# Two-layer Fourier and attention block on one core: a norm's chain, column operations, the special columns' product and a fourth weight buffer

## The chip, the core and the metric

The kernel runs on one core of a Trainium2 chip. The core has five engines, each with an instruction queue of its own: TensorE (PE, matrix products; its weight loads are shown as PEld), VectorE (DVE), ScalarE (ACT), GpSimd (POOL) and SyncE (SP, which here only issues DMAs). On-chip memory is SBUF, and products are accumulated in eight banks of PSUM. The metric is the device time of one execution in microseconds.

## The reference, cut to what matters

Two layers work on 256 tokens `x` and 256 context tokens `ctx`, each of 2048 features. Layer 0 is a Fourier mixer on both, layer 1 is windowed attention. All is float32.

```python
shift, scale, gate = split(silu(c) @ ada_w[i] + ada_b[i], 3)
h = rmsnorm(x, norm_g[i]) * (1 + scale) + shift            # the same for ctx with c_ctx
# layer 0:
u, z = split(h @ w_in, 2)                                   # 4096 features each
ug = u.reshape(b, n, 16, 256)                               # 16 groups of 256 features
f = fft2(ug, axes=(tokens, group features), norm='ortho').real
f = einsum('bngc,gcd->bngd', f, w_mix).reshape(b, n, 4096)
y = f * silu(z)
x = x + gate * (y @ w_out[0])
# layer 1: the same with attention in place of the Fourier branch, then a final rmsnorm
```

The change lies in layer 0, in the first 200 us of the time.

## The kernel before, in words

**Numbers in halves.** Each float32 operand is split into two parts of a shorter float type: `split` (lines 60 to 62) copies the high part on ACT (L61) and subtracts it on DVE (L62). `mm3` (L73 to L76) makes three products, high by high (L74), high by low (L75), low by high (L76).

**The opening** (L331 to L379). Four blocks of 128 rows `xn` are loaded: two of `x` (s = 0), two of `ctx` (s = 1). `square` sums squares, one half of the features on ACT, the other on DVE. `xsplit(t, c)` splits 512 features of block t. `turn_x` transposes a block pair on PE into PSUM (L236), where the first call takes all eight banks, and `copy_x` copies the banks out, even ones on DVE (L244), odd ones on ACT (L242). `norm(s)` (L196 to L208) adds the sums (L200), takes the inverse root in `rsqrt` (L78 to L87: L82 on DVE, the power on POOL in L83, three small DVE steps), scales the table `dm` of the token transform into the splits `dh` (ACT, L205) and `dl` (DVE, L206), and copies the root to `rr` (L207). `dft(s, c)` then makes the transform over tokens with `dh` and `dl` as the moving side (L74 to L76, `ps<-dh,xs`). `ada` (L249 to L254) makes pieces of the modulation from `awp`, 1 MB loads; `turn` (L261 to L273) turns them and writes the scale `gs0` (L271) and the shift `sh0` (L269).

**The z products** (L390 to L441), four steps of four feature tiles k. `z_x(k)` scales the turned tokens (L303), makes the split of the modulated tokens on ACT (L304) and DVE (L305, `zl_end`); `z_step(k)` multiplies them by the weights of the first six blocks of z. `hx_prep(k)` (L316 to L328) makes `hx`, the split of the token transform for the u products (L322 on ACT, L323 on DVE), and puts the value with the shift in it into column 0 (`f0` in L324, then L326 and L327). At the end the six sums go through Silu (L440) to memory as `zd`, on POOL's queue.

**The sixteen groups** (L483 to L553). `load_u(g)` loads the two 1 MB halves of group g's folded weights (`raw`, L47), forms differences and sums (`wm` in L123, L124) and splits them (`wml`, `wmh`, `wpl`, `wph`) into eight tiles of pool `wfp`. `load_m(g)` loads the group's mixing matrix `m` (group 0 on POOL's queue, others on ACT's), forms `mt` (L458, L459), and multiplies it by the feature transform tables `ch`, `cl`. `part` multiplies `hx` by the group's weights: part m (48 products of 256 columns), then part p (48 of 260). `mix` joins the results of the group before. In group 0 the special columns (features 0 and 128 of every group, `wsp`, 32 in all) are multiplied by `hx` once: 16 tiles, three products each, with 32 stationary columns (L514 to L518); their result goes into `asp` (L519 to L521), which `mix` reads. `load_m(0)` is written ahead of this loop (L479).

**Buffers.** Loads of weights go through `raw`, three buffers of 8 KB a partition (L35), in the opening also through two more (`raw_st`). Pools that are opened with `reuse_waits="tile"` lie where closed pools lay, and their tiles wait for the tiles that lay there before. `ext` (14 tiles of 2 KB) holds splits of the z products and the Silu results until they are stored.

**The order of the work.** The text is one stream. A planner with a time model of its own puts each engine's instructions in an order when the program is built: what the model finds ready first, earlier text before later. `tc.issue_after(ins)` adds that instructions of the same engine as `ins`, written in its block, stand behind `ins` in that engine's queue; instructions of other engines in the block are not bound. On the chip each queue runs strictly in that order.

Of the kernel before, what the change touches and what calls it, by code (L numbers as in the profile page):

```python
# [29 lines left out]
def tile_dit(ctx: ExitStack, tc: tile.TileContext, a: dict, out: bass.AP):  # L30
# [21 lines left out]
    def act(dt=F32):  # L52
        return actp.tile([P, 512], dt, tag="act", name="act")
# [24 lines left out]
    def rsqrt(pool, src, w, tag):  # L78
# [3 lines left out]
        V.tensor_scalar(v, src, 1.0 / D, EPS, op0=ALU.mult, op1=ALU.add)  # L82
# [52 lines left out]

    def load_u(g):
        return [split_uh(*f) for f in [load_uh(g, kh) for kh in range(2)]]
# [13 lines left out]
    with tc.tile_pool(name="st", reuse_waits="tile", bufs=1, side="right") as st, ExitStack() as sts:  # L151
# [44 lines left out]
        def norm(s):  # L196
# [4 lines left out]
            r = rsqrt(st, s2, 2, f"r{s}")  # L201
# [94 lines left out]
        zl_end = [None]  # L296

        def z_x(k):
            h, l = ext(F32R), ext(F32R)
            for s in range(2):  # L300
# [4 lines left out]
                zl_end[0] = V.scalar_tensor_tensor(l[:, q], t, sh0[:, k, s : s + 1], h[:, q].bitcast(F32), op0=ALU.add, op1=ALU.subtract).ins  # L305
# [10 lines left out]
        def hx_prep(k):  # L316
            i, kk = k // 2, k % 2
            h, l = act(F32R), act(F32R)
            for s in range(2):
# [4 lines left out]
                V.scalar_tensor_tensor(f0[:, k, s : s + 1], rw[:, 0:1], gs0[:, k, s : s + 1], sh16[:, k, s : s + 1], op0=ALU.mult, op1=ALU.add)  # L324
            h, l = (x.rearrange("p (s j) -> p s j", s=2) for x in (h, l))
            V.tensor_copy(h[:, :, 0], f0[:, k, :])  # L326
            V.tensor_tensor(l[:, :, 0], f0[:, k, :], h[:, :, 0].bitcast(F32), op=ALU.subtract)  # L327
# [8 lines left out]
        norm(0)  # L336
        xsplit(1, 0)
        for kp in range(4):
            copy_x(0, kp, ox[kp])
        xsplit(1, 1)  # L340
        dft(0, 0)
        for kp in range(4, 8):
            copy_x(0, kp, ox[kp])
        xsplit(0, 2)
        xsplit(1, 2)
        square(2)
# [43 lines left out]
        for i in range(4):  # L390
            k = 4 * i
            for j in range(4):
                z_x(k + j)
                if j == 1:
                    zl_two = zl_end[0]
                if j == 0:
                    with tc.issue_after(zl_end[0]):
                        hx_prep(k)
# [15 lines left out]
            else:  # L414
                with tc.issue_after(zl_two):
                    wur = [load_uh(0, kh, raw_st) for kh in range(2)]
# [30 lines left out]
    sph, spl = act(F32R), act(F32R)  # L447
    split(sph, spl, wsr)
# [30 lines left out]
    m0 = load_m(0)  # L479
    fd = [dram.tile([P, 512], F32, name=f"fd{b}") for b in range(NB)]  # L480
    up = us.enter_context(tc.tile_pool(name="up", reuse_waits="tile", bufs=2))
    asp = up.tile([96, 2, 130], F32R, name="asp", bufs=1)
    for g in range(G):  # L483
# [29 lines left out]
        if g == 0:  # L513
            osp = psum()[0:32, 0:260].rearrange("p (s j) -> p s j", s=2)  # L514
            for k in range(KT):
                h, l = hx[k]
                q = slice(k * 32, (k + 1) * 32)
# [733 lines left out]
```

## Time and profile before

| | us |
|---|---|
| median of three runs | 1862.07 (1858.95 to 1866.89) |
| the profiled execution | 1863.31 |
| span of its instructions | 1861.5 |
| PE busy | 1824.5 (98%) |
| DVE busy | 1412.0 (76%) |
| ACT busy | 976.5 (52%) |

The span runs from the first to the last instruction; the profiled execution's own time is 1.8 us longer. L12 is line 12 of the kernel. In a timeline row stand start, duration, engine, line, operation, tiles written and read, sizes and, in brackets, the idle time of the engine ahead of it and what ended that. Groups of instructions have busy time, mean duration in ns and idle time. An engine's wait is put down to what came last. Products are pipelined, so that their durations overlap: the distance of their starts is what one costs.

### The profile page before, as it was taken

To read this page: it belongs to the slowest core of one execution; us is meant where nothing else is said; L and a number is where in the kernel's file an instruction comes from. 1 tells how busy PE (TensorE), PEld (TensorE's weight loads), DVE (VectorE), ACT (ScalarE), POOL (GpSimd) and SP (SyncE) were. 2 spreads that over 40 slices of the span, in tenths; PEclk is the share of its full clock that TensorE was granted. 3 is DMA by queue.
4 is the path that set the end of the run, shared out by engine and by line. 5 is a ranking of instruction groups with operands and counts; after the bars stand their busy time and mean duration, and the time that the engine had idled before them with its cause. 6 is when DMAs were issued, how large, how long until landed. Compare 5 with 4: busy or idle time off the path is not lost.

```text
span 1861.5 us, 26287 instructions
## 1 busy us (share of the span) xinstructions
PE 1824.5 (98%) x9953; PEld 1555.9 (84%) x9953; DVE 1412.0 (76%) x2406; ACT 976.5 (52%) x1713; POOL 158.7 (9%) x182
## 2 busy tenths in 40 slices
PE   7998999999999999999999999999999999999997
PEld 6658999998888888888888787888888888887886
DVE  5657999978897898578964825888878878887454
ACT  6445444444222243224222624888888888896343
POOL 0001000020000000000000001111220220300010
PEclk9999999999999999999999999999999999999999
DMA  7984565585766756654675324333333333434543
GB/s 314 362 355 148 196 209 197 188 287 204 299 259 228 277 197 256 257 216 165 228 265 215 114 94 147 123 135 132 118 120 130 136 117 133 159 136 181 186 176 136
DMA packets 63934, 362.74 MB, mean 195 GB/s; under 512 B 7744, under 2 KB 7888, under 8 KB 29504
## 3 DMA queue, kind: packets, MB, share of 16 engines
q1 hardware_dynamic: 52448, 326.67, 48.0%
q0 software_dynamic: 7472, 27.71, 4.0%
q10 hardware_dynamic: 3888, 6.69, 1.2%
q8 instruction: 78, 1.28, 0.3%
q14 instruction: 48, 0.39, 0.1%
HBM read 346.87 MB, written 14.16 MB: 194 GB/s over the span
## 4 chain that ended last, share of the span: by engine, by line
PE 93%; DVE 2%; DMA 2%; ACT 2%; issue 1%; POOL 0%; ACTq 0%; POOLq 0%; SPq 0%; DVEq 0%
PE ps L74 24%; PE ps L75 24%; PE ps L76 24%; PE ps L950 6%; PE ps L952 3%; PE ps L1006 3%; PE ps L1021 2%; PE ps L1020 2%; PE ps L986 2%; PE ps L987 1%; PE ps L254 1%; DMA m<-in_wm 1%; DMA raw<-in_awp 0%; DVE wl L62 0%; PE ps L236 0%
## 5 line engine op out<-in xcount | busy, mean ns | idle before, releaser
L61 ACT CAST wh<-raw 128x1024 fp32r<-128x1024 f32 x329 | 345.0, 1051 | 457.6 <-PE ps L75 348.6
L62 DVE TENSOR_TENSOR wl<-raw,wh 128x1024 fp32r<-128x1024 f32 x329 | 415.9, 1267 | 200.0 <-ACT wh L61 197.4
L75 PE MATMUL ps<-act,wh 128*128 128x512 f32 x928 | 361.0, 389 | 0.0
L74 PE MATMUL ps<-act,wh 128*128 128x512 f32 x928 | 357.9, 389 | 0.0
L76 PE MATMUL ps<-act,wl 128*128 128x512 f32 x928 | 356.6, 389 | 0.8 <-DVE wl L62 0.8
L76 PEld LDWEIGHTS ps<-act,wl 128*128 128x128 f32 x928 | 174.2, 188 | 37.3 <-DVE wl L62 1.2
L75 PEld LDWEIGHTS ps<-act,wh 128*128 128x128 f32 x928 | 174.2, 188 | 36.0
L74 PEld LDWEIGHTS ps<-act,wh 128*128 128x128 f32 x928 | 174.2, 188 | 35.9
L950 PE MATMUL ps<-h,wh 128*128 128x512 f32 x512 | 187.0, 400 | 0.0
L579 DVE CUSTOM_DVE_ANT_0 raw<-raw,cb 128x1024 f32<-128x1024 f32 x128 | 154.8, 1220 | 33.7 <-DMA raw<-in_adw 32.7
L579 DVE CUSTOM_DVE_ANT_0 junk<-raw,cb 128x1024 f32<-128x1024 f32 x96 | 117.1, 1220 | 29.4 <-DMA raw<-in_adw 16.1
L952 PE MATMUL ps<-h,wl 128*128 128x256 f32 x512 | 138.1, 280 | 0.0
L75 PE MATMUL ps<-wl,h 128*128 128x512 f32 x320 | 126.1, 394 | 1.5 <-DVE wl L62 1.5
L74 PE MATMUL ps<-wh,h 128*128 128x512 f32 x320 | 124.8, 398 | 0.2 <-ACT h L769 0.2
L76 PE MATMUL ps<-wh,h 128*128 128x512 f32 x320 | 124.5, 391 | 0.0
L950 PEld LDWEIGHTS ps<-h,wh 128*128 128x128 f32 x512 | 96.2, 188 | 19.0
L988 DVE CUSTOM_DVE_ANT_0 ps<-ps,mask,nsink 128x512 f32<-128x512 f32 x128 | 92.1, 754 | 12.3 <-PE ps L987 11.3
L991 ACT ACTIVATE p<-ps,mx 128x512 f32<-128x512 f32 x128 | 87.3, 687 | 24.8 <-DVE mx L988 24.2
L952 PEld LDWEIGHTS ps<-h,wl 128*128 128x128 f32 x512 | 96.8, 189 | 1.4
L62 DVE TENSOR_TENSOR pl<-ps,ph 128x512 fp32r<-128x512 f32 x128 | 83.7, 685 | 10.0 <-ACT ph L61 8.8
L996 ACT ACTIVATE p<-p,sm 128x512 f32<-128x512 f32 x128 | 85.4, 717 | 7.9 <-DVE sm L994 7.8
L75 PE MATMUL ps<-wl,ys 128*128 128x512 f32 x212 | 83.3, 393 | 0.0
(323 smaller groups left out, 3790.6 us busy)
## 6 DMA issues: line engine op xcount, KB each, us to landing
raw<-in_adw SPq DMA_DIRECT2D x64, 1024.0 KB, 5.1
raw<-in_wz SPq DMA_DIRECT2D x62, 1024.0 KB, 4.9
raw<-in_awp SPq DMA_DIRECT2D x32, 1024.0 KB, 8.0
raw<-in_wo SPq DMA_DIRECT2D x32, 1024.0 KB, 5.6
raw<-in_wq SPq DMA_DIRECT2D x32, 1024.0 KB, 4.8
raw<-in_wu SPq DMA_DIRECT2D x32, 1016.0 KB, 5.4
raw<-in_wo1b SPq DMA_DIRECT2D x16, 1024.0 KB, 4.9
act<-in_xT POOLq DMA_DIRECT2D x32, 256.0 KB, 5.2
```

The costliest lines, as they stand in the source:

```text
L61: S.copy(h, src)
L62: V.tensor_tensor(l, src, h.bitcast(F32), op=ALU.subtract)
L74: PE.matmul(o, wh, xh, start=start, stop=False)
L75: PE.matmul(o, wh, xl, start=False, stop=False)
L76: PE.matmul(o, wl, xh, start=False, stop=stop)
L579: V.tensor_tensor_reduce(junk if s == 0 and i < 3 else wf, wf, cb[:, s], 1.0, 0.0, ALU.mult, ALU.add, acc[:, i, kh, fg * 2 + f, s : s + 1])
L950: PE.matmul(o[0], wh[:, q], hx1[k], start=k == 0, stop=k == KT - 1)
L952: PE.matmul(o[0][:, 0:N], wl[:, q], hx1[k][:, 0:N], start=False, stop=False)
L988: V.tensor_tensor_reduce(o, o, mask[:, tb, :], -0.125, nsink[:, i : i + 1], ALU.add, ALU.min, mx[:, tb : tb + 1])
L991: S.activation(pt[:, tb, :], so[tb], AF.Exp, bias=mx[:, tb : tb + 1], scale=-1.0, accum_out=sm[:, tb : tb + 1])
L996: S.activation(pt[:, tb, :], pt[:, tb, :], AF.Copy, scale=sm[:, tb : tb + 1])
L1006: PE.transpose(o[:, (kt * 2 + tb) * P : (kt * 2 + tb + 1) * P], pt[:, tb, c : c + P], ident)
```

## The change

It has five parts.

1. In `norm(0)`, `rsqrt` takes a function that it calls after its first DVE step, with issue order behind that step; `xsplit(1, 0)` goes there. What the opening does next, up to `square(2)`, stands in DVE's queue behind the copy to `rr`.
2. In `hx_prep` the operations on column 0 move behind the last DVE split of `z_x(k + 1)`, or of the step's last tile. The first `hx_prep(k)` of each step no longer waits for `z_x(k)`'s last split; it is written behind all four `z_x`.
3. The special columns' high and low weights lie side by side in one stationary operand of 64 columns. Two products a tile (with the high and the low part of `hx`) replace three; the product of the two low parts is now in the sum. The lower half of the result is copied out on ACT and added to the upper one on DVE.
4. `load_m(0)` is written behind the special columns' product, and its products stand behind it in PE's queue.
5. Each fourth load of `load_u` goes to a buffer `rawu` of its own (8 KB a partition); its pool lies ahead of `up` among the pools of the group stage.

```diff
--- before.py
+++ after.py
@@ -75,11 +75,13 @@
         PE.matmul(o, wh, xl, start=False, stop=False)
         PE.matmul(o, wl, xh, start=False, stop=stop)
 
-    def rsqrt(pool, src, w, tag):
+    def rsqrt(pool, src, w, tag, between=lambda: None):
         v = pool.tile([P, w], F32, tag=tag + "v", name=tag + "v")
         t = pool.tile([P, w], F32, tag=tag + "s", name=tag + "s")
         r = pool.tile([P, w], F32, tag=tag + "r", name=tag + "r")
-        V.tensor_scalar(v, src, 1.0 / D, EPS, op0=ALU.mult, op1=ALU.add)
+        vi = V.tensor_scalar(v, src, 1.0 / D, EPS, op0=ALU.mult, op1=ALU.add).ins
+        with tc.issue_after(vi):
+            between()
         GP.tensor_tensor(r, v, mhalf[:, 0:w], op=ALU.pow)
         V.tensor_tensor(t, r, r, op=ALU.mult)
         V.scalar_tensor_tensor(t, t, -0.5, v, op0=ALU.mult, op1=ALU.mult)
@@ -133,8 +135,18 @@
             fl[nm] = (h, l)
         return fl
 
+    def raw_u(src):
+        ucnt[0] += 1
+        if ucnt[0] % 4:
+            return raw(src)
+        t = rawu.tile([P, D], F32, tag="rawu", name="rawu")
+        nc.sync.dma_start(t[:, : src.shape[-1]], src)
+        return t
+
+    ucnt = [0]
+
     def load_u(g):
-        return [split_uh(*f) for f in [load_uh(g, kh) for kh in range(2)]]
+        return [split_uh(*f) for f in [load_uh(g, kh, raw_u) for kh in range(2)]]
 
     lay0 = ctx.enter_context(ExitStack())
     adap = lay0.enter_context(tc.tile_pool(name="ada", bufs=1))
@@ -193,12 +205,12 @@
                 else:
                     V.tensor_tensor_reduce(dump, x, x, 1.0, 0.0, ALU.mult, ALU.add, ss[:, t, c : c + 1])
 
-        def norm(s):
+        def norm(s, between=lambda: None):
             q = slice(2 * s, 2 * s + 2)
             s2 = st.tile([P, 2], F32, name=f"s2{s}")
             with tc.issue_after(rend[0]) if s else nullcontext():
                 V.tensor_reduce(s2, ss[:, q, :], axis=AX.X, op=ALU.add)
-            r = rsqrt(st, s2, 2, f"r{s}")
+            r = rsqrt(st, s2, 2, f"r{s}", between)
             dh = sx.tile([P, 2, N], F32R, name=f"dh{s}")
             dl = sx.tile([P, 2, N], F32R, name=f"dl{s}")
             for tt in range(2):
@@ -293,7 +305,7 @@
                 ]
 
         zx = {}
-        zl_end = [None]
+        z_l = {}
 
         def z_x(k):
             h, l = ext(F32R), ext(F32R)
@@ -302,7 +314,7 @@
                 t = xT[k // 2][s][:, (k % 2) * N : (k % 2 + 1) * N]
                 V.scalar_tensor_tensor(t, t, gs0[:, k, s : s + 1], r_bc[:, q], op0=ALU.mult, op1=ALU.mult)
                 S.activation(h[:, q], t, AF.Identity, bias=sh0[:, k, s : s + 1])
-                zl_end[0] = V.scalar_tensor_tensor(l[:, q], t, sh0[:, k, s : s + 1], h[:, q].bitcast(F32), op0=ALU.add, op1=ALU.subtract).ins
+                z_l[k] = V.scalar_tensor_tensor(l[:, q], t, sh0[:, k, s : s + 1], h[:, q].bitcast(F32), op0=ALU.add, op1=ALU.subtract).ins
             zx[k] = (h, l)
 
         def z_step(k, bs=range(NE)):
@@ -321,10 +333,12 @@
                 rw = rawx[i][s][:, kk * N : (kk + 1) * N]
                 S.activation(h[:, q], rw, AF.Copy, scale=gs0[:, k, s : s + 1])
                 V.scalar_tensor_tensor(l[:, q], rw, gs0[:, k, s : s + 1], h[:, q].bitcast(F32), op0=ALU.mult, op1=ALU.subtract)
-                V.scalar_tensor_tensor(f0[:, k, s : s + 1], rw[:, 0:1], gs0[:, k, s : s + 1], sh16[:, k, s : s + 1], op0=ALU.mult, op1=ALU.add)
             h, l = (x.rearrange("p (s j) -> p s j", s=2) for x in (h, l))
-            V.tensor_copy(h[:, :, 0], f0[:, k, :])
-            V.tensor_tensor(l[:, :, 0], f0[:, k, :], h[:, :, 0].bitcast(F32), op=ALU.subtract)
+            with tc.issue_after(z_l[min(k + 1, k // 4 * 4 + 3)]):
+                for s in range(2):
+                    V.scalar_tensor_tensor(f0[:, k, s : s + 1], rawx[i][s][:, kk * N : kk * N + 1], gs0[:, k, s : s + 1], sh16[:, k, s : s + 1], op0=ALU.mult, op1=ALU.add)
+                V.tensor_copy(h[:, :, 0], f0[:, k, :])
+                V.tensor_tensor(l[:, :, 0], f0[:, k, :], h[:, :, 0].bitcast(F32), op=ALU.subtract)
             hx.append((h, l))
 
         early, late = range(NE // 2), range(NE // 2, NE)
@@ -333,17 +347,17 @@
         xsplit(0, 1)
         ox = turn_x(0, range(8))
         square(1)
-        norm(0)
-        xsplit(1, 0)
-        for kp in range(4):
-            copy_x(0, kp, ox[kp])
-        xsplit(1, 1)
-        dft(0, 0)
-        for kp in range(4, 8):
-            copy_x(0, kp, ox[kp])
-        xsplit(0, 2)
-        xsplit(1, 2)
-        square(2)
+        norm(0, lambda: xsplit(1, 0))
+        with tc.issue_after(rend[0]):
+            for kp in range(4):
+                copy_x(0, kp, ox[kp])
+            xsplit(1, 1)
+            dft(0, 0)
+            for kp in range(4, 8):
+                copy_x(0, kp, ox[kp])
+            xsplit(0, 2)
+            xsplit(1, 2)
+            square(2)
         dft(0, 1)
         square(3)
         xsplit(0, 3)
@@ -391,11 +405,7 @@
             k = 4 * i
             for j in range(4):
                 z_x(k + j)
-                if j == 1:
-                    zl_two = zl_end[0]
-                if j == 0:
-                    with tc.issue_after(zl_end[0]):
-                        hx_prep(k)
+            hx_prep(k)
             if i < 3:
                 ada(i + 1, 1, 0)
                 ada(i + 1, 1, 1)
@@ -412,7 +422,7 @@
                 ada(i + 1, 0, 0)
                 ada(i + 1, 0, 1)
             else:
-                with tc.issue_after(zl_two):
+                with tc.issue_after(z_l[k + 1]):
                     wur = [load_uh(0, kh, raw_st) for kh in range(2)]
             hx_prep(k + 2)
             if i == 2:
@@ -444,8 +454,11 @@
     mk = cload("mk", [96, G], pool=adap)
     wsr = wsp.tile([P, 512], F32, tag="ws", name="wsr")
     nc.gpsimd.dma_start(wsr, a["wsp"])
-    sph, spl = act(F32R), act(F32R)
-    split(sph, spl, wsr)
+    sphl = []
+    for i in range(2):
+        t = act(F32R).rearrange("p (k c) -> p k c", c=64)
+        split(t[:, :, 0:32], t[:, :, 32:64], wsr[:, i * 256 : (i + 1) * 256].rearrange("p (k c) -> p k c", c=32))
+        sphl.append(t)
 
     ua = us.enter_context(tc.tile_pool(name="ua", reuse_waits="tile", bufs=2))
 
@@ -476,8 +489,8 @@
 
     parts = (("m", 128, 256), ("p", 0, 130))
 
-    m0 = load_m(0)
     fd = [dram.tile([P, 512], F32, name=f"fd{b}") for b in range(NB)]
+    rawu = us.enter_context(tc.tile_pool(name="rawu", reuse_waits="tile", bufs=1))
     up = us.enter_context(tc.tile_pool(name="up", reuse_waits="tile", bufs=2))
     asp = up.tile([96, 2, 130], F32R, name="asp", bufs=1)
     for g in range(G):
@@ -511,15 +524,19 @@
             mix()
             part(parts)
         if g == 0:
-            osp = psum()[0:32, 0:260].rearrange("p (s j) -> p s j", s=2)
+            o2 = psum()[0:64, 0:260].rearrange("p (s j) -> p s j", s=2)
             for k in range(KT):
-                h, l = hx[k]
-                q = slice(k * 32, (k + 1) * 32)
-                mm3(osp, sph[:, q], spl[:, q], h[:, :, 0:130], l[:, :, 0:130], k == 0, k == KT - 1)
+                for x_ in hx[k]:
+                    sp_end = PE.matmul(o2, sphl[k // 8][:, k % 8], x_[:, :, 0:130], start=k == 0 and x_ is hx[k][0], stop=k == KT - 1 and x_ is hx[k][1]).ins
+            osl = up.tile([32, 2, 130], F32, name="osl", bufs=1)
+            S.copy(osl, o2[32:64])
+            osp = up.tile([32, 2, 130], F32, name="osp", bufs=1)
+            V.tensor_tensor(osp, o2[0:32], osl, op=ALU.add)
             S.copy(asp[0:32], osp)
             S.copy(asp[64:96], osp)
             V.tensor_tensor(asp[32:64], osp, asp[0:32].bitcast(F32), op=ALU.subtract)
-            pqh, pql, sp = m0
+            with tc.issue_after(sp_end):
+                pqh, pql, sp = load_m(0)
         mh, ml = am[g % 2]
         split(mh[0:127, :, 1:128], ml[0:127, :, 1:128], oa["m"][:, :, 1:128])
         if g < G - 1:
```

## The prediction

> **What bounds the kernel now.** I read the page first: its engine rows and the chain that ended last.
>
> ```profile
> span 1861.5 us, 26287 instructions
> ...
> PE 1824.5 (98%) x9953; PEld 1555.9 (84%) x9953; DVE 1412.0 (76%) x2406; ACT 976.5 (52%) x1713; POOL 158.7 (9%) x182
> ...
> PE 93%; DVE 2%; DMA 2%; ACT 2%; issue 1%; POOL 0%; ACTq 0%; POOLq 0%; SPq 0%; DVEq 0%
> ```
>
> TensorE is the bound, and 93% of the chain is its own work. So an edit can gain only by taking products away or by closing a place where PE stands idle. Next I asked who PE waits for in the first 200 us, which hold every place that the diff touches, and how the stages around it are loaded.
>
> ```profile
> PE ps L236 <- DMA xn<-in_x: 6.9, 1, 6.9
> PE ps L74 <- ACT dh L205: 2.8, 1, 2.8
> PE ps L76 <- DVE wml L62: 1.9, 1, 1.9
> PE ps L74 <- ACT ext L304: 1.9, 2, 1.4
> PE ps L75 <- DVE ml L62: 1.6, 1, 1.6
> PE ps L74 <- ACT mh L61: 1.2, 1, 1.2
> ...
> 60.00:120.00 60.00, 59.15 (x334) 35.56 (x333) 37.99 (x120) 27.62 (x56) 0.60 (x1) 1.00 0.98 392
> 200.00:380.00 180.00, 180.00 (x1496) 180.00 (x1495) 172.08 (x242) 87.48 (x165) 13.19 (x25) 1.00 0.59 201
> ```
>
> The wait rows are: who waited, us in total, times, longest. The window rows give PE, PEld, DVE, ACT, POOL, granted clock, DMA share and GB/s. From 200 to 380 PE has no gap at all, so time won before 200 should reach the end, as long as DVE keeps up: it is busy 172.08 of 180 us there (96%). From 60 to 120 the DMA engines are 98% busy, but the loads there are issued as PE releases buffers; if PE comes earlier, they do too.
>
> **The change, part by part.** *(a) Norm's chain.* The timeline of the opening:
>
> ```profile
> 6.91 6.13 PE L236 MATMUL ps<-ident,xn 128*128 128x128 f32 x32 [6.91 <-DMA xn<-in_x]
> ...
> 11.02 0.69 DVE L244 COPY act<-ps 128x512 f32<-128x512 f32 x1
> ...
> 11.63 0.15 DVE L200 TENSOR_REDUCE s<-ss 128x2 f32<-128x4 f32 x1
> 11.69 0.68 DVE L62 TENSOR_TENSOR xs<-xn,xs 128x512 fp32r<-128x512 f32 x1
> ...
> 12.69 1.06 ACT L192 ACTIVATE dump<-xn 128x1024 f32<-128x1024 f32 x1
> ...
> 13.21 1.01 POOL L83 TENSOR_TENSOR r0r<-r0v,mhalf 128x2 f32<-128x2 f32 x1 [10.73 <-DVE r0v L82]
> ...
> 14.71 0.15 DVE L84 TENSOR_TENSOR r0s<-r0r 128x2 f32<-128x2 f32 x1
> ...
> 15.29 0.91 ACT L205 ACTIVATE dh<-dm,r0r 128x256 fp32r<-128x256 f32 x2 [1.45 <-DVE r0r L86]
> ...
> 15.85 1.23 PE L74 MATMUL ps<-dh,xs 128*128 128x256 f32 x4 [2.81 <-ACT dh L205]
> ...
> 17.96 0.16 DVE L200 TENSOR_REDUCE s<-ss 128x2 f32<-128x4 f32 x1
> ...
> 18.40 0.70 POOL L83 TENSOR_TENSOR r1r<-r1v,mhalf 128x2 f32<-128x2 f32 x1 [4.18 <-DVE r1v L82]
> ...
> 19.73 0.91 ACT L205 ACTIVATE dh<-dm,r1r 128x256 fp32r<-128x256 f32 x2 [2.50 <-DVE r1r L86]
> ```
>
> Between the sum at 11.63 and `dh` at 15.29 stand DVE copies, splits and a square. The second norm, undisturbed, takes 17.96 to 19.73, 1.77 us. With the copy at 11.02 gone to behind the chain, the sum starts at about 11.0; with 0.3 us more because the power runs beside a DVE split (1.01 us at 13.21 against 0.70 at 18.40), `dh` comes at 13.1 and PE starts 0.56 us later, at 13.7 instead of 15.85. Against that 2.2 us: the copies, which free PSUM, now come after the chain (0.7 us each), and ACT's square at 12.69 may stand ahead of `dh`. I take **1.6**; the ends are 0 (PE waits for a bank instead) and 2.8, all of the idle time. Three DVE instructions of 0.7 us and the square move behind; PE is then still in its first products, which covers them. Without that cover they cost up to 3 us.
>
> *(b) Column operations.* Their count stays; they move behind the next token block's last split. Each `f0` operation takes 213 ns on DVE.
>
> ```profile
> L324 DVE SCALAR_TENSOR_TENSOR f<-act,gs,sh 128x1 f32<-128x1 f32 x32 | 5.5, 213 | 0.1
> ```
>
> PE's waits nearby (1.9 us on `ext`) are for ACT, which starts when the shift arrives, so I take **0**; the ends are +1.9 and −0.9 (four such operations ahead of what PE waits for). The cover at the end is 3 us: the columns are first read by the special product.
>
> *(c) The first `load_m`, behind the special product.* Its products now stand early in PE's order and cause the waits on `mh` (1.2) and `ml` (1.6). Its 13 products stay; behind them on PE queues part p of group 0, and its input is long there by then (the row of POOL below). **2.8**; ends 0 and 2.8.
>
> *(d) The special columns* fall from 48 products to 32; POOL's, PE's and DVE's rows of this joint:
>
> ```profile
> 145.21 0.55 POOL L454 DMA_DIRECT2D m<-in_wm  x1
> 163.41 0.28 PE L74 MATMUL ps<-act 128*32 128x260 f32 x1
> ...
> 169.06 0.28 PE L76 MATMUL ps<-act 128*32 128x260 f32 x1
> ...
> 179.10 0.28 PE L74 MATMUL ps<-act,wmh 128*127 128x256 f32 x1
> ...
> 153.62 10.35 DMA m<-in_wm
> 164.06 0.42 DVE L458 TENSOR_TENSOR mt<-m 128x256 f32<-128x256 f32 x1 [3.21 <-DMA m<-in_wm]
> 165.86 1.21 DVE L62 TENSOR_TENSOR wml<-wm,wmh 128x1016 fp32r<-128x1016 f32 x1
> 171.19 5.23 DMA raw<-in_wu
> 172.21 1.04 ACT L61 CAST wmh<-wm 128x1016 fp32r<-128x1016 f32 x1 [2.09 <-PE ps L75]
> 176.45 1.22 DVE L123 TENSOR_TENSOR wm<-raw 128x1016 f32<-128x1016 f32 x1 [4.38 <-DMA raw<-in_wu]
> 180.17 1.21 DVE L62 TENSOR_TENSOR wml<-wm,wmh 128x1016 fp32r<-128x1016 f32 x1
> 181.44 0.39 PE L76 MATMUL ps<-act,wml 128*127 128x256 f32 x1 [1.93 <-DVE wml L62]
> ...
> 188.05 1.22 DVE L123 TENSOR_TENSOR wm<-raw 128x1016 f32<-128x1016 f32 x1 [2.25 <-DMA raw<-in_wu]
> ```
>
> First to last of 48 is 5.65 us, 0.12 each; 16 fewer give **1.9** (at 127 stationary columns PE's products take 0.28 too, so that 64 should not cost more). The added ACT copy and DVE sum of the two halves (under 0.5 us each, as L458's 0.42 for 256 columns) delay `asp`, which PE first reads in `mix`, after part m of group 1.
>
> *(e) The fourth buffer.* The row at 176.45 is why it matters: DVE stands 4.38 us for a load issued at 171.19, when a buffer came free, and the split that PE lacks at 181.44 is queued behind it, though ACT's half was ready at 173.25. With a buffer of its own that load can go as soon as the memory under it is free (by tile sizes it lies over `ext` tiles, of which the last stores land near 165), so it lands by about 170. After the wait the clock falls too:
>
> ```profile
> 182.00:184.00 2.00, 2.00 (x14) 2.00 (x13) 2.00 (x3) 0.78 (x1) 0.00 (x0) 0.65 0.00 0
> 184.00:186.00 2.00, 2.00 (x11) 2.00 (x11) 1.74 (x3) 0.59 (x1) 0.00 (x0) 0.50 0.90 260
> ```
>
> A granted clock of 0.65 and 0.50 over 2 us each loses 0.7 + 1.0 = 1.7 us, so the place costs 1.9 + 1.7 = 3.6. But (c) and (d) bring PE here 4.7 us earlier, so that its wait would begin not at 179.5 (181.44 less 1.93) but at 174.8. DVE has from 164.06 (after `m`, whose load is not helped) to 181.4 as its list, 17.3 us, 4.4 of them the wait; without it the split ends at 177.0 at the old order, 2.2 us late, and at 173 to 175, in time, if the planner puts it ahead of the work for group 2. I take the middle, about half of the 3.6: **1.8**; the ends are 3.6 and −4.7 (DVE not earlier at all, so that PE gives (c) and (d) back).
>
> The Trainium skill, "TensorE: Matmul & The Clock Gate", section "HAM oscillation — how this bites in real kernels", has only idle gaps above about 3.4 us throttle the clock. By that rule the place costs its idle time alone, the term would be about 0.9 and the sum 7.2 in place of 8.1; the row shows the fall after 1.93 us, and I go by the row.
>
> **Sum.** 1.6 + 0 + 2.8 + 1.9 + 1.8 = 8.1 us. The profiled execution took 1863.3 us, 1.2 above the median of the three runs; against the median 1862.1 the forecast is **1854.0 us**, −0.44%. From no change I could tell about 0.5%, 9.3 us: a time under 1852.8 is faster, one over 1871.4 slower.
>
> **The rivals.** *R1: DVE's queue takes the wait over.* For: DVE's list above, and `m` of group 1 landing 10.35 us after its issue, beside 1 MB loads and the `zd` stores; one more load in flight, sharing by bytes, adds 1 MB at 392 GB/s, 2.7 us, to it and to all behind it. Against: DVE idles 3.21 and 4.38 us here, room to reorder. If the split ends at 179.7, (c) to (e) yield the 1.7 us between that and 181.4 and the clock still falls: 1.6 + 1.7 = 3.3, 1858.8 us. The Trainium skill, "DMA: Bandwidth & Descriptors", section "Queues, rings and completion order", says that a DMA engine goes round its queues packet by packet. By that rule a longer queue on SP would not delay ACT's `m`, and the sum would stay 8.1; no row here shows `m` beside a longer queue.
>
> *R2: everything closes.* (a) 2.8, (b) 1.9, (c) 2.8, (d) 1.9, (e) 3.6: 13.0 us, 1849.1. Against it: it needs a planner's order without any new wait.
>
> *R3: the opening gains nothing*, since PE waits for a PSUM bank that a copy behind the chain frees: 8.1 − 1.6, 1855.6 us.
>
> *R4: slower, by DVE in the groups.* The planner, given a fourth buffer, may put the sums of the next group (L123) ahead of the splits that PE needs, and DVE stand there for the load in every group, as at 188.05 (2.25 us).
>
> ```profile
> L454 ACTq DMA_DIRECT2D m<-in_wm x7: 334/334/335, 211.6 to 296.5; - x7
> ```
>
> A group takes (296.5 − 211.6) / 6 = 14.15 us, DVE 96% of it, 13.5. A wait of 2.25 makes a group 15.8, 1.6 more in each of 14: 22 less 8 gives +14, 1876 us. It loses from 0.6 + 8.1 / 14 = 1.2 us a group on. Against: now PE has no gap in these groups, and a buffer more makes loads earlier.
>
> **How the numbers follow.** The forecast holds 0.50 (its own range 1851 to 1857.5), R1 0.20, R2 0.12, R3 0.10, R4 0.08. Faster by over 0.5%: R2 nearly whole and a third of the forecast, with a little of R3, 0.29. Slower by over 0.5%: the worse part of R4, 0.05. Within: 0.66. The range 1848.5 to 1862.5 leaves out R4, the edge of R2 and little of R1.
>
> **What would show it.** (a): `dh` before 13.5 and the first L74 before 14.3. (c): no PE wait on `mh` or `ml` from 150 to 165. (d): 32 products with 64 columns, under 3.9 us. (e): the weight load of group 2's second half issued before 166, DVE's waits for `in_wu` gone, PE's wait on `wml` under 1 us, a granted clock of 1.00 behind it. Wrong it would be by new PE gaps between 20 and 60 us, by DVE waits in the groups, or by a wait moved to the next `m`.

## The result and the profile after

The changed kernel takes **1855.8 us** (median of six runs, 1854.0 to 1856.8) against 1861.7 (six runs, 1859.0 to 1866.9): a ratio of 0.9964, 95% interval 0.9953 to 0.9975. The forecast was 1854.0, the range 1848.5 to 1862.5; by the bound of 0.5% it is the same, which had 0.66. In a second comparison (e9 below) the ratio was 0.9962 [0.9948, 0.9976]. So the kernel is some 6 to 7 us faster. The two profiled executions differ by more, 9.4 us of span, because the one of after was the quickest of its six and the one of before lay above its median.

The page of after, its span, its engines and the shares of its chain:

```profile
span 1852.2 us, 26279 instructions
...
PE 1818.5 (98%) x9937; PEld 1551.0 (84%) x9937; DVE 1411.5 (76%) x2408; ACT 975.7 (53%) x1715; POOL 158.7 (9%) x182
...
PE 88%; DMA 3%; DVE 3%; issue 3%; ACT 2%; POOL 0%; ACTq 0%; POOLq 0%; SPq 0%; DVEq 0%
```

PE has 16 instructions less and 6.0 us less busy time, and stays the bound. Its waits in the first 200 us of after (waiting line, releaser, us in total, times, longest):

```profile
PE ps L248 <- DMA xn<-in_x: 6.5, 1, 6.5
PE ps L266 <- DMA raw<-in_awp: 3.2, 4, 1.4
PE ps L74 <- ACT ext L316: 1.9, 2, 1.4
PE ps L74 <- ACT dh L217: 1.2, 1, 1.2
PE ps L276 <- ACT rows L270: 1.1, 1, 1.1
PE ps L75 <- DVE dl L218: 1.1, 1, 1.1
PE ps L75 <- DVE ml L62: 0.3, 1, 0.3
```

The waits on `mh` (1.2), `wml` (1.9) and nearly all of that on `ml` (1.6) are gone, and `dh` has fallen from 2.8 to 1.2. One is new, 1.1 for `dl`. One has grown to 3.2 us, that for the loads of the modulation weights, which in before was:

```profile
PE ps L254 <- DMA raw<-in_awp: 0.8, 2, 0.5
```

The stage from 60 to 120 and the place where the clock fell, as windows of after (us, busy time of PE, PEld, DVE, ACT, POOL, granted clock, DMA share, GB/s). PE is some 8 us ahead of before there, so that the products at 182 to 186 in before stand at 174 to 178:

```profile
60.00:120.00 60.00, 57.10 (x320) 34.44 (x319) 35.12 (x116) 24.20 (x49) 0.60 (x1) 1.00 0.92 371
174.00:176.00 2.00, 2.00 (x19) 2.00 (x18) 1.94 (x3) 1.04 (x1) 0.00 (x0) 1.00 0.00 0
176.00:178.00 2.00, 2.00 (x19) 2.00 (x19) 1.97 (x4) 0.00 (x0) 0.00 (x0) 1.00 0.00 0
```

The clock is 1.00 where it was 0.65 and 0.50 (and in every window of 2 us from 160 to 200). But PE is busy 57.10 of the 60 us, where it was 59.15. To see what each stretch brought I compared the starts of products of equal kind and number. Two pairs, first in before, then in after: the product on `dh` near 38 us, and the last z product.

```profile
38.52 0.36 PE L74 MATMUL ps<-dh,xs 128*128 128x256 f32 x1
...
153.03 0.39 PE L76 MATMUL ps<-ext 128*128 128x512 f32 x1
```

```profile
36.09 0.37 PE L74 MATMUL ps<-dh,xs 128*128 128x256 f32 x1
...
153.06 0.40 PE L76 MATMUL ps<-ext 128*128 128x512 f32 x1
```

So the opening gained 2.43 us, and **the whole of it was gone at the end of the z products** (+0.03). From there to the products at 194 us (of before) after gains 8.3 us: 2.8 for `mh` and `ml`, 1.9 for sixteen products, 1.9 for `wml` and 1.7 for the clock make 8.3, to within the 0.3 us that PE now waits on the next group's `ml`. Of the other 1.1 us, 0.9 is chance in the granted clock at one later place that the change doesn't touch, here first in before, then in after:

```profile
1035.00:1045.00 10.00, 7.87 (x30) 6.77 (x31) 5.76 (x17) 4.75 (x11) 1.03 (x1) 0.66 0.83 287
```

```profile
1026.00:1036.00 10.00, 7.62 (x36) 6.65 (x36) 5.32 (x16) 5.05 (x11) 1.03 (x1) 0.83 0.87 301
```

The sum of the prediction came out right, but not its terms: the opening, put at 1.6, gave nothing, and the place at 180 us, put at 1.8, gave its whole 3.6. The runs had to say why.

### The profile page after: what moved, and what is told of

It reads as the page before. It is cut to its first block, busy times and chain, and to the rows that moved or that the text cites. A ratio compares the mean times of both kernels' runs of the same rounds, so it can differ in the third digit from the quotient of the medians.

```text
span 1852.2 us, 26279 instructions
## 1 busy us (share of the span) xinstructions
PE 1818.5 (98%) x9937; PEld 1551.0 (84%) x9937; DVE 1411.5 (76%) x2408; ACT 975.7 (53%) x1715; POOL 158.7 (9%) x182
## 4 chain that ended last, share of the span: by engine, by line
PE 88%; DMA 3%; DVE 3%; issue 3%; ACT 2%; POOL 0%; ACTq 0%; POOLq 0%; SPq 0%; DVEq 0%
PE ps L75 22%; PE ps L74 22%; PE ps L76 22%; PE ps L967 6%; PE ps L969 3%; PE ps L1023 3%; PE ps L1038 2%; PE ps L1037 2%; PE ps L1003 2%; PE ps L1004 2%; PE ps L266 1%; DMA raw<-in_awp 1%; DMA act<-in_xT 1%; DVE wl L62 1%; DMA raw<-in_adw 1%
```

## The experiments

All runs were timed against the kernel before on the same chip. The table has the ratio with its interval, and from the profiled execution of each, against that of before, the shift of the last z product and of the end of the span (negative is earlier).

| run | parts in it | ratio | last z product | end |
|---|---|---|---|---|
| the change | 1 to 5 | 0.9964 [0.9953, 0.9975] | +0.03 | −9.4 |
| e1_norm_only | 1 | 0.9992 [0.9983, 1.0002] | −0.4 | −4.5 |
| e2_columns_only | 2 | 0.9999 [0.9990, 1.0008] | +1.9 | +0.4 |
| e3_special_only | 3, 4 | 0.9947 [0.9933, 0.9962] | −0.4 | −10.5 |
| e4_buffer_only | 5 | 0.9993 [0.9983, 1.0002] | −1.4 | −2.8 |
| e5_without_columns | 1, 3, 4, 5 | 0.9957 [0.9942, 0.9972] | −0.1 | −10.1 |
| e6_without_buffer | 1, 2, 3, 4 | 0.9966 [0.9953, 0.9979] | +3.4 | −7.8 |
| e7_products_only | 3 | 0.9970 [0.9960, 0.9979] | +1.8 | −4.1 |
| e8_place_only | 4 | 0.9966 [0.9953, 0.9979] | +0.2 | −8.3 |
| e9_changed_again | 1 to 5 | 0.9962 [0.9948, 0.9976] | −0.7 | −10.4 |
| e10_norm_whole | 1 (longer), 3, 4 | 0.9966 [0.9953, 0.9978] | +1.8 | −8.3 |
| e11_half_loads | 3, 4, half loads | 0.9967 [0.9954, 0.9980] | +3.3 | −7.4 |
| e12_half_loads_norm | 1, 3, 4, half loads | 0.9962 [0.9947, 0.9977] | +2.5 | −6.0 |

One execution differs from the next by 2 us and more, so the columns from the traces tell where time goes; what a version is worth is told by the ratio.

### Part 1 alone

```diff
-        norm(0)
-        xsplit(1, 0)
...
+        norm(0, lambda: xsplit(1, 0))
+        with tc.issue_after(rend[0]):
...
```

> The kernel before with the norm's chain alone (part 1). Loads theory: the DMA engines cannot deliver the opening's loads sooner, so the first product comes at 13.7 us in place of 15.85, but the z products end near 153.3 us as in both kernels, and the time stays within 1 us of before. Order theory: it is part 2 that gives the 2.4 us back, by putting the modulation products behind more z products; then without part 2 the z products end near 150.9 us and the time falls by about 2.4 us.

Measured 1862.49 us, 0.9992 [0.9983, 1.0002]: nothing that can be told from no change. The first product came 1.54 us earlier, but PE still waited 2.0 for `dh` and then 1.1 for `dl`, and the clock was low for longer (0.74, 0.50 and 0.90 from 16 to 22 us, in before 0.84, 0.50 and 0.81 from 14 to 20), so that near 38 us only 0.28 was left and at the last z product 0.41. The waits on `mh`, `ml` and `wml` (1.2, 1.5, 1.7) stayed. The 4.5 us at the end of this execution are not the opening's: after the wait on `wml` its clock happened to stay at 1.00, and the rest came later in the kernel. Part 1 pays nothing by itself.

### Part 2 alone

```diff
...
-                if j == 0:
-                    with tc.issue_after(zl_end[0]):
-                        hx_prep(k)
+            hx_prep(k)
...
```

> The kernel before with the column operations' move alone (part 2). Loads theory: end of the z products at 153.3 us, no change of the time. Order theory: in TensorE's queue the first three modulation products' tiles of a step stand 12 or so z products later than before, the buffers come free later, TensorE waits for awp some 2 to 3 us more in all, the z products end at 155 to 156 us and the time rises by 2 to 3 us.

Measured 1863.32 us, 0.9999 [0.9990, 1.0008]. Of PE's waits in the first 200 us of this run, that for the modulation weights is 3.4 us where it was 0.8, that on `wml` is longer than in before (1.9), and that on `ml` (1.6) is gone:

```profile
PE ps L254 <- DMA raw<-in_awp: 3.4, 3, 1.4
PE ps L76 <- DVE wml L62: 2.4, 1, 2.4
```

A lead of 0.5 us at 59 us (the first load happened to land earlier) is a lag of 1.9 at the last z product: 2.4 us lost. No DVE operation on column 0 is what PE waits for. The order that the planner gives PE is another: with `hx_prep(k)` written behind all four `z_x`, 31 z products stand ahead of the first step's modulation products and not 24 (in the fourth step it is six more), so that the buffers they read come free later, the loads behind them start later, and PE waits for these. That is a price outside both ends I had given. It doesn't reach the end: of the 1.9 us only 0.1 is left at the end of group 0's part m, since PE no longer waits there for `ml`.

### Parts 3 and 4 alone

```diff
-    m0 = load_m(0)
...
-                mm3(osp, sph[:, q], spl[:, q], h[:, :, 0:130], l[:, :, 0:130], k == 0, k == KT - 1)
+                for x_ in hx[k]:
+                    sp_end = PE.matmul(o2, sphl[k // 8][:, k % 8], x_[:, :, 0:130], start=k == 0 and x_ is hx[k][0], stop=k == KT - 1 and x_ is hx[k][1]).ins
...
+            with tc.issue_after(sp_end):
+                pqh, pql, sp = load_m(0)
```

> The kernel before with the special columns in 32 products and the first mixing matrix behind them (parts 3 and 4), no fourth buffer. If the fourth buffer is what lets TensorE keep this gain: the waits on mh and ml go, the group's part p starts 4.7 to 5 us earlier, but the wait on wml in group 1 grows from 1.9 to 4 us or more, the clock falls behind it, and no more than 2.5 us remain. If the buffer is not needed: the wait stays at 2 us or less and 4.7 us or more remain.

Measured **1853.06 us**, 0.9947 [0.9933, 0.9962]. These two parts give the whole gain. The wait on `wml` is gone without the fourth buffer, and the clock holds (PE is some 9 us ahead here; it is 1.00 in every window of 2 us from 160 to 200):

```profile
172.00:174.00 2.00, 2.00 (x19) 2.00 (x19) 1.94 (x4) 1.63 (x4) 0.00 (x0) 1.00 0.33 46
174.00:176.00 2.00, 2.00 (x19) 2.00 (x19) 1.97 (x3) 0.64 (x2) 0.00 (x0) 1.00 0.22 85
```

The load for group 2's second half went out at 162.46 us through an ordinary buffer, where in before it was 171.19: with `load_m(0)` behind the special product, DVE reaches the split `wpl` of group 1, the last reader of that buffer, at 161.2 and not at 169.95.

### Part 5 alone

```diff
-        return [split_uh(*f) for f in [load_uh(g, kh) for kh in range(2)]]
+        return [split_uh(*f) for f in [load_uh(g, kh, raw_u) for kh in range(2)]]
```

> The kernel before with the fourth weight buffer alone (part 5). If VectorE's wait for the late load is the cause: the load of group 2's second half is issued before 166 us, the wait of 4.4 us on it goes, TensorE's wait on wml (1.9 us) goes and the granted clock stays at 1.00 from 182 to 186, so that the profiled execution loses 3.6 us. If VectorE's list itself is too long: the wait on wml stays near 1.9 us and the time too.

Measured 1862.47 us, 0.9993 [0.9983, 1.0002]. The buffer does its part: its load goes out at 156.74 and lands at 165.19, and DVE no longer stands 4.38 us for it but 1.53 for the next one. PE no longer waits at this place, the clock stays at 1.00, and from the last z product to 193 us this run gains 3.3 us. But one group later PE waits again, here in the list of its waits and in its timeline:

```profile
PE ps L75 <- DVE apl L62: 1.2, 1, 1.2
...
PE ps L76 <- DVE wml L62: 0.7, 1, 0.7
```

```profile
193.66 0.38 PE L76 MATMUL ps<-act,wml 128*127 128x256 f32 x1 [0.73 <-DVE wml L62]
...
198.33 0.39 PE L75 MATMUL ps<-apl,pqh 127*128 127x260 f32 x1 [1.20 <-DVE apl L62]
```

0.7 and 1.2 are together what 1.9 was, but at other places: the wait moved on by a group, and of the 4.7 us that this run was ahead at 193, 2.4 were gone by 200. (The 1.4 us that it was ahead at the last z product came from the opening, where its clock happened to hold.)

### The whole change without part 2

```diff
-            hx_prep(k)
...
+                if j == 0:
+                    with tc.issue_after(zl_end[0]):
+                        hx_prep(k)
...
```

> The changed kernel with part 2 undone (column operations and hx_prep where they stood before), parts 1, 3, 4 and 5 in. Order theory: the z products end about 2.4 us sooner than in the changed kernel, TensorE's waits for awp fall from 3.2 us to about 1, and the time falls by some 2.4 us to about 1853.4. Loads theory: the z products end near 153 us all the same and the time stays at 1855.8.

Measured 1853.73 us, 0.9957 [0.9942, 0.9972], against 0.9964 with it: not to be told apart. In the trace the opening's lead now lives longer, 2.54 us at 59, 2.38 at 83 and at 109. From 126 us on it is lost at one place: PE waits 2.43 us for a load that was issued at 120.40 and landed at 129.10, 4.9 us behind the one before it, where neighbours are 2.5 apart. What held that load up is not shown. So part 2 is not the only taker.

### The whole change without part 5

```diff
-        return [split_uh(*f) for f in [load_uh(g, kh, raw_u) for kh in range(2)]]
+        return [split_uh(*f) for f in [load_uh(g, kh) for kh in range(2)]]
```

> The changed kernel with the fourth weight buffer undone. If parts 3 and 4 close the wait on wml by themselves, as they did alone: wait on wml under 0.5 us, granted clock 1.00 from 170 to 186, the time within 1 us of the changed kernel's. If the buffer carries it here: the load of group 2's second half is issued some 8 us later, the wait on wml comes back with 2 us, the clock falls, and the time is 3 us or more above the changed kernel's.

Measured 1855.47 us, 0.9966 [0.9953, 0.9979]. There is no wait on `wml`, the clock is 1.00 from 180 to 188, and the load of group 2's second half goes out at 165.09. The fourth buffer adds nothing that can be measured once parts 3 and 4 are there.

### Part 3 alone, part 4 alone

Only the products, with `load_m(0)` where it was; and only the place of `load_m(0)`, with 48 products:

```diff
+                for x_ in hx[k]:
+                    sp_end = PE.matmul(o2, sphl[k // 8][:, k % 8], x_[:, :, 0:130], start=k == 0 and x_ is hx[k][0], stop=k == KT - 1 and x_ is hx[k][1]).ins
```

> The kernel before with the 32 products (part 3) alone, the first mixing matrix at its old place. Place theory: the saving is 16 products of 0.12 us, 1.9 us, the waits on mh and ml stay (2.8), the wait on wml stays or grows, and the time falls by no more than 2 us. Rival, the special columns' product itself holds the group's start: 5 us or more.

```diff
-    m0 = load_m(0)
...
-            pqh, pql, sp = m0
+            with tc.issue_after(sp_end):
+                pqh, pql, sp = load_m(0)
```

> The kernel before with the first mixing matrix behind the special columns' product (part 4) alone, still 48 products. Place theory: the waits on mh and ml go (2.8 us), group 0's part m ends 3 us sooner, so that VectorE makes group 1's wpl before 166 us, the load behind it is issued before 166 us in place of 171.2, the wait on wml (1.9 us) and the fall of the clock (1.7 us) go: 6 to 8 us in all. Rival, only the two waits go: 2.8 us, and the wait on wml grows.

Part 3 alone: 1856.75 us, 0.9970 [0.9960, 0.9979]. Part 4 alone: 1854.99 us, 0.9966 [0.9953, 0.9979]. I had held the place to be what closes the wait on `wml`, and part 3 to be worth its 1.9 us; part 3 is worth 5.6 [3.9, 7.5]. The waits on `mh` and `ml` are still there (1.2 and 1.9), but that on `wml` is gone, though the load goes out only at 173.18, later than in before. DVE's timeline in this run shows how:

```profile
176.70 1.22 DVE L62 TENSOR_TENSOR wml<-wm,wmh 128x1016 fp32r<-128x1016 f32 x1 [1.53 <-ACT wmh L61]
178.64 1.22 DVE L123 TENSOR_TENSOR wm<-raw 128x1016 f32<-128x1016 f32 x1 [0.72 <-DMA raw<-in_wu]
```

The split that PE needs now stands **ahead** of the sum that waits for the load; in before it stands behind it (176.45 and 180.17 in the rows of the prediction). So there are two ways to close this place, an earlier load (part 4) or another order in DVE's queue (part 3), and each is enough. By that, part 3 is worth 1.9 + 3.6 = 5.5, part 4 is worth 2.8 + 3.6 = 6.4, and both together 8.3, not 11.9; measured were 5.6, 6.3 and 9.9 [7.1, 12.5] us. (Of the 3.6, the clock's 1.7 is what the profiled execution of before lost; e1, with nearly the same wait, lost nothing of it.)

### The change once more, a longer part 1, and half loads

Four runs on one chip. e9 is the change itself:

> The change whole once more, beside the version below on one chip. Expected: 1855.8 us, between 1854 and 1857, as before. It is here so that the version with parts 1, 3 and 4 alone is compared with it on the same chip and not over two.

Measured 1857.35 us, 0.9962 [0.9948, 0.9976], with the opening's lead at 2.25 us from 38 to 57 and 0.7 left at the last z product.

In e10 the whole of norm's chain comes first, `dl` too, and two copies go into the place where the power runs; parts 2 and 5 are left out:

```diff
-                V.scalar_tensor_tensor(dl[:, tt], dm[:, tt], r[:, tt : tt + 1], dh[:, tt].bitcast(F32), op0=ALU.mult, op1=ALU.subtract)
-            rend[0] = V.tensor_copy(rr[:, q], r).ins
+                rend[0] = V.scalar_tensor_tensor(dl[:, tt], dm[:, tt], r[:, tt : tt + 1], dh[:, tt].bitcast(F32), op0=ALU.mult, op1=ALU.subtract).ins
+            V.tensor_copy(rr[:, q], r)
...
+        def between():
+            xsplit(1, 0)
+            copy_x(0, 0, ox[0])
+            copy_x(0, 1, ox[1])
+
+        norm(0, between)
```

> Parts 1, 3 and 4 without 2 and 5, and with the whole of norm's chain first: the split that makes dl comes ahead of the copies too, the copy of r behind it, and the first two copies go into the place where the power runs. Theory (DVE's queue order in the opening): the first product about 13.3 us, and the wait of 1.1 us on dl gone, so that the products on dl start at about 13.7 (16.29 with the change). Theory (the loads of the modulation weights set the end of the z products): the 2.2 us are gone again at 153 all the same, and the time is that of parts 3 and 4 alone, 1853 us (1852 to 1854). Rival (the opening's gain is lost to part 2's order, not to the loads): z's end 2.0 to 2.4 us earlier than before, and 1850.5 to 1851.5 us.

Measured 1856.35 us, 0.9966 [0.9953, 0.9978]. The opening does what was expected, and more: `dh` at 12.81, the first product at 13.37, no wait on `dl`, no cold clock, and a lead of 3.45 us near 38 (this is the product shown above at 38.52 and 36.09). Then comes this, in the same run's timeline of PE, the granted clock behind it, and the last z product:

```profile
35.07 0.36 PE L74 MATMUL ps<-dh,xs 128*128 128x256 f32 x1
...
63.75 2.78 PE L256 MATMUL ps<-raw,c 128*32 128x512 f32 x24
...
77.13 3.30 PE L256 MATMUL ps<-raw,c 128*32 128x512 f32 x16 [3.90 <-DMA raw<-in_awp]
...
154.86 0.40 PE L76 MATMUL ps<-ext 128*128 128x512 f32 x1
```

```profile
76.00:78.00 2.00, 0.87 (x7) 0.21 (x10) 0.00 (x0) 0.00 (x0) 0.00 (x0) 0.64 0.97 410
78.00:80.00 2.00, 2.00 (x16) 0.38 (x8) 0.00 (x0) 0.00 (x0) 0.00 (x0) 0.51 1.05 442
```

PE stands 3.90 us for a load, and the clock falls behind that. The load's piece of the chain in e10, and the row of before that answers to the products at 63.75:

```profile
66.63 10.46 DMA raw<-in_awp
```

```profile
63.83 2.78 PE L254 MATMUL ps<-raw,c 128*32 128x512 f32 x24
```

The 24 modulation products that free three buffers start at 63.75 us in e10 and at 63.83 in before: the same time, though PE is 3.45 us ahead. The last tile that they read had landed 4.4 us earlier in e10 (59.34), and 1.0 us earlier in before (62.81); in between PE does z products that in before come later. The loads that go into the freed buffers, and the next one behind them, then land one behind the other, 2.49 us apart, at the same moments in both: 69.64, 72.12, 74.59, 77.09 in e10, and 69.64, 72.14, 74.62, 77.11 in before. So the lead was used up in z products done early, and when those were out PE had to wait for loads that had not moved. In the change the same batch went out at 64.09 and landed 0.8 us earlier, for a lead of 2.43.

Did the loads fail to move because they can't come sooner, or because PE's order was another? The traces of the other runs tell these apart. The same 24 products in e4 and in e5, which have the order of before in this step:

```profile
62.12 2.78 PE L264 MATMUL ps<-raw,c 128*32 128x512 f32 x24
```

```profile
61.27 2.78 PE L266 MATMUL ps<-raw,c 128*32 128x512 f32 x24
```

| run | z products ahead of the 24 | the 24 start | first load behind them lands | lead near 38 us | lead left at 82 | at the last z product |
|---|---|---|---|---|---|---|
| before | 24 | 63.83 | 69.64 | | | |
| e4 | 24 | 62.12 | 68.28 | 1.69 | 1.41 | 1.41 |
| e5 | 24 | 61.27 | 67.16 | 2.54 | 2.38 | 0.09 |
| the change | 31 | 62.97 | 68.89 | 2.43 | 0.79 | −0.03 |
| e2 | 31 | 64.91 | 70.98 | 0.50 | −1.32 | −1.91 |
| e10 | 39 | 63.75 | 69.64 | 3.46 | −2.20 | −1.83 |

Where the order is that of before, the products and the loads behind them come earlier by nearly the whole lead, and most of the lead is still there at 82 us. Where the planner put 7 or 15 z products more ahead of them, it is lost there. The rest of the z products has such places too: in e5 the order first differs in the fourth step, behind 109 us, and the lead is lost behind that (e1 has that order too, and its lead of 0.3 stayed). The order isn't all: e7 has that of before throughout and falls 0.9 us further behind at 78.

And does the size of the loads matter? e11 and e12 halve the loads of the later three steps (the half that is loaded is used twice, so the second half of these weights is left out of the computation), without and with part 1:

```diff
-            t = raw_st(a["awp"][which, i, kg])
+            t = raw_st(a["awp"][which, i, kg][:, 0 : 1024 if i else D])
...
```

> Parts 3 and 4 alone, with the loads of the modulation weights of the later three steps at half their size; each half tile is used twice, so that the second half of these weights is left out of the computation. It is the base for the next one. Loads theory: no wait of PE on these loads; the end of the z products is earlier than with parts 3 and 4 whole (where it is 0.35 us before that of the kernel before) by at most the waits that are left there, up to 3 us; the time 1850 to 1853 us. Rival (the waits come from the order of the work, not from the loads' size): the same as parts 3 and 4 whole, 1853 us.

> The same with half loads, and part 1 (norm's chain first) with them. Loads theory: the opening's gain is now kept: the z products end 1.5 to 2.5 us earlier than with half loads alone, and the time is 1.5 to 2.5 us less. Rival (something else than the loads takes the gain: PSUM banks, DVE or ACT between 20 and 150 us): the difference at z's end is below 0.7 us, and the times agree within 0.7 us.

Measured 1855.87 and 1856.22 us, 0.9967 [0.9954, 0.9980] and 0.9962 [0.9947, 0.9977]. Neither theory had this: with half the bytes the z products end not earlier, but 3.3 and 2.5 us later than in before. With the loads changed the planner changed PE's order too, and put modulation products ahead of z products where their tile was not there yet (none of the 24 z products of before stands ahead of the first ones). PE's timeline in e11, and one of its windows:

```profile
56.35 1.06 PE L254 MATMUL ps<-raw,c 128*32 128x512 f32 x8
60.48 4.48 PE L254 MATMUL ps<-raw,c 128*32 128x512 f32 x24 [3.06 <-DMA raw<-in_awp]
```

```profile
40.00:60.00 20.00, 16.28 (x132) 11.58 (x130) 11.01 (x33) 12.13 (x25) 0.00 (x0) 1.00 0.58 198
```

PE waits 3.06 us for a load with the DMA engines 58% busy, so a load's size alone does not make these waits. As a pair the runs are not conclusive: in e12 the clock was cold until 23 us, so that it entered the z products later than e11, by 0.8 us at 38, and left them 0.8 earlier. A run that holds PE's order and changes only the loads was not made.

## Why the prediction was right, and where its steps were not

**The total** was 1.8 us off the median. The terms were not all right; two errors of opposite sign, −1.6 and +1.8, met, and that is luck.

**(a) Norm's chain, 1.6: failed.** The times of the step itself came true. After's timeline of the opening (start, duration, engine, line, operation; in brackets the idle time ahead):

```profile
12.74 0.91 ACT L217 ACTIVATE dh<-dm,r0r 128x256 fp32r<-128x256 f32 x2 [1.56 <-DVE r0r L88]
...
12.82 1.28 DVE L256 COPY act<-ps 128x512 f32<-128x512 f32 x2
...
13.65 0.35 PE L74 MATMUL ps<-dh,xs 128*128 128x256 f32 x1 [1.16 <-ACT dh L217]
...
14.62 1.22 DVE L206 CUSTOM_DVE_ANT_0 dump<-xn 128x1024 f32<-128x1024 f32 x1
...
15.76 0.88 DVE L218 SCALAR_TENSOR_TENSOR dl<-dm,r0r,dh 128x256 fp32r<-128x256 f32 x2
...
16.29 0.39 PE L75 MATMUL ps<-dl,xs 128*128 128x256 f32 x1 [1.11 <-DVE dl L218]
```

`dh` at 12.74 and the first product at 13.65 are the forecast's 13.1 and 13.7. I overlooked `dl`: it is a DVE instruction behind the copy to `rr` as well, and the planner put it behind two copies, a split and the square, at 15.76; PE got its first product on `dl` only 0.6 us earlier than before (16.87). Of the 2.43 near 38 us, 0.7 more came by 20 us, where after's clock stays at 1.00 and before's does not (of the seven profiled executions with part 1 it held in four and fell in e1, e6 and e12), and 1.1 between 28 and 38, where PE's order has sixteen modulation products in one piece and not in two. So what the chain itself gave PE was 0.6, and not 1.6. That alone would have been mended by e10. What failed then is the sentence that time won before 200 us should reach the end: from 200 on PE has no gaps, but between 60 and 153 the place of the modulation products in PE's order set the pace. "If PE comes earlier, they do too" held for the loads where the planner kept its order (2.5 us earlier at the first of them in e5, 1.4 in e4) and failed where it made another: 0.8 us in the change, and in e10 the same times to 0.03 us. The prediction took the order as given.

**(b) Column operations, 0 in [−0.9, +1.9]: failed in the trace, not in the time.** e2 loses 2.4 us by the last z product, through PE's planned order, which I had not considered: I counted DVE instructions. The ratio of e2 is 0.9999, because there the loss ends in PE's wait on `ml`; and with and without part 2 the change can't be told apart. So the price isn't seen at the end.

**(c) `load_m(0)`, 2.8, and (d) the special columns, 1.9: right.** Waits on `mh` none and on `ml` 0.3 in after. (The step counts 13 products in `load_m`; the traces have ten. No term rests on it.) At the joint:

```profile
158.34 0.33 SPq L143 DMA_DIRECT2D rawu<-in_wu  x1
...
159.00 4.00 PE L530 MATMUL ps<-act 128*64 128x260 f32 x32
...
162.84 0.28 PE L74 MATMUL ps<-mh,ch 128*128 128x256 f32 x1
...
172.31 1.22 DVE L125 TENSOR_TENSOR wm<-rawu 128x1016 f32<-128x1016 f32 x1
173.44 1.21 DVE L62 TENSOR_TENSOR wml<-wm,wmh 128x1016 fp32r<-128x1016 f32 x1
```

32 products take 3.84 us to the next start, 0.12 each: 64 stationary columns cost what 32 did.

**(e) The fourth buffer, 1.8 in [−4.7, 3.6]: the effect right, the cause wrong.** Everything that was to show it came: the load at 158.34, no DVE wait for it, no wait on `wml`, a clock of 1.00, 3.6 us in all. But e3 and e6 have all of that without the buffer, and e4, with the buffer alone, closes the place but gains nothing measurable, because the wait comes back a group later. The step said that (c) and (d) bring PE there 4.7 us earlier and make its wait longer; I had priced them on PE alone. Each of them also takes work out of the way of DVE and of the buffers, and closes the wait by itself. The load went out at 158.34 (156.74 in e4), and not after 165: the memory under `rawu` was free before the last stores landed (164.59).

**The rivals.** R1, DVE's queue taking the wait over, did not happen in the change, but in e4 it did: all of the 1.9 us came back at 193 to 198, 0.7 on `wml` and 1.2 on `apl`. `m` of group 1 landed 7.9 us after its issue in after (156.34 to 164.23), against 10.35 before; in e4, with the buffer alone, it took 10.3 (152.20 to 162.52), and in e3, without it, 8.5. The Trainium skill, "DMA: Bandwidth & Descriptors", section "Queues, rings and completion order", says that a DMA engine serves its queues in turn, packet by packet; these rows agree with it in so far as the longer SP queue did not delay ACT's load. R3 gave 1855.6 us, next to what was measured, and its outcome (the opening gains nothing) was right with another mechanism: PE waits for loads between 73 and 85 us, not for a PSUM bank. R4 had no trace: DVE is busy 168.10 us of the 180 from 200 to 380 in after, PE 180.00.

**What stays open**: whether the opening's lead would reach the end of the z products if PE kept the order of before in all four steps; with it, e4 kept 1.4 of 1.7 us, but from a lead that came by chance, and e5 kept 2.4 of 2.5 only as far as its order was the same. A kernel with part 1 and a held order was not tried, nor was what makes the planner put the modulation products later. The best version is not settled either: parts 3 and 4 alone have the lowest ratio, 0.9947 [0.9933, 0.9962], but its interval overlaps that of the whole change.

## What to carry to other kernels

Before counting a gain in an early stage, look for the next stage that is paced by loads, and ask whether those loads' issue really moves with the engine: here a lead of 3.45 us met loads that landed within 0.03 us of their old times, because the planner had put 15 products more ahead of what frees their buffers; with the old order they moved with the engine. Two edits that remove the same wait share its price, so that price each edit alone and then the pair (5.5 and 6.4 gave 8.3). And in a kernel whose order a planner makes, an edit is also a change of order elsewhere: read the new order of the queues before pricing instructions.

## What the runs showed of the hardware that was not expected

Whether the clock falls after an idle time of PE is not told by its length alone. In the opening e4 idles 3.22 us ahead of its first product and keeps a granted clock of 1.00, while e3 idles 3.71 and falls; before fell with 2.81. From 16 to 20 us, e4 and then e3:

```profile
16.00:18.00 2.00, 2.00 (x19) 2.00 (x18) 1.71 (x5) 0.77 (x2) 0.07 (x1) 1.00 0.97 406
18.00:20.00 2.00, 2.00 (x19) 2.00 (x18) 0.86 (x5) 0.75 (x2) 0.63 (x1) 1.00 1.03 426
```

```profile
16.00:18.00 2.00, 2.00 (x12) 2.00 (x11) 1.78 (x5) 0.84 (x2) 0.00 (x0) 0.58 0.99 414
18.00:20.00 2.00, 2.00 (x12) 2.00 (x12) 0.79 (x5) 0.68 (x2) 0.70 (x1) 0.57 1.04 430
```

That is 1.7 us of work, by luck. At 180 us the clock fell after waits of 1.93 (before) and 2.4 us (e2), not after 1.7 (e1); in e10 it fell at 77 us after 3.90. The Trainium skill, "TensorE: Matmul & The Clock Gate", section "Part 1: The HAM clock gate (the "warmup" mystery)", says that activity is watched in a free-running window of about 3.4 us. That waits of like length ended one way in one run and the other way in another agrees with that. Its section "HAM oscillation — how this bites in real kernels" gives as the rule "no PE-idle gaps >~3.4µs"; here gaps of 1.93, 2.4 and 2.81 us were followed by a fall, so staying below that was not enough, and the measurement decides.
